# Where the last input forms of the gates and of the up projection are made, and at which offset the first weights of a block lie

## The chip, the cores and the metric

The kernel runs on one core of a Trainium2 chip. A core has TensorE (matmuls), VectorE, ScalarE, GpSimd and the queues that issue DMAs (SyncE's among them); each works through its own list of instructions in order, and they meet at semaphores. The metric is the device time of one execution in microseconds (us). The profile names the engines PE (its weight loads PEld), DVE, ACT, POOL and SP.

## The reference, cut to what matters

One layer of an encoder, 512 tokens of width 2048, all in float32:

```python
h = rmsnorm(x, norm_mix)
qa, ka, va, qb, kb, vb, ga, gb = split(h @ w_in)      # ga, gb: 2048 columns each
out_a = window_attention(...);  out_b = neighbourhood_attention(...)
merged = sigmoid(ga) * (out_a @ w_branch_a) + sigmoid(gb) * (out_b @ w_branch_b)
x = x + merged @ w_out
u = rmsnorm(x, norm_ffn) @ w_up                       # 2048 x 11264
u = depthwise_conv_of_width_3(u) + conv_b
gate, val = split(u)
x = x + (silu(gate) * val) @ w_down                   # 5632 x 2048
```

## The kernel before

**Precision.** A float32 number is kept as two parts of the type float32r: the high one (a cast on ScalarE) and the low one, what is left (a subtraction on VectorE). A product is made of three matmuls: high by high, high by low, low by high. So every 128-row tile of weights has to be split before TensorE can use it: L634 and L635 for the blocks described next, L735 and L736 for the others.

**Blocks of products.** From the fourth block of 512 gate columns on, the gates, the whole up projection and most of the down projection use seven products in place of eight: the work on two 128-row slices of the contraction, two halves of 256 columns and two halves of 256 tokens is taken as a 2 x 2 by 2 x 2 product, and seven sums of its quarters are multiplied (the method of Strassen and Winograd). One such piece is a *unit* (the class Product): 7 sums x 2 column tiles x 3 matmuls = 42 matmuls with 256 moving columns. Eight units, one for each pair of slices, make a block of up or of the gates, which holds seven PSUM banks. There are 5 blocks of gates (the first is called block 3), 22 of up, and 12 of down, of which 3 (PLAIN) go the ordinary way with all eight products. The weights' sums are partly made on VectorE (L589 to L593), partly fetched ready from DRAM.

**The forms of the input.** The other operand, seven sums of a pair of input slices, is called the pair's forms. They are made once and used by all blocks: eight pairs for the gates (hf, by form_h) and eight for up (h2, by form_pair). One pair costs one instruction of 512 and two of 256 columns on VectorE (L663, L665, L666), seven casts on ScalarE (L675) and seven subtractions on VectorE (L676), all of 256 columns. Before that, ScalarE scales the two slices by the norm's weights (L861 in scale_x, L976 in scale_pair). form_h(j) also has GpSimd issue the load of x's slices j + 2 (L854) and issues scale_x(j + 1). The seven forms lie in seven of 56 slots.

**Where the forms are made.** For the gates: while TensorE works on gate block 2, the last in the ordinary layout, whose input hT lies in the slots; before its steps 0 to 5 and 7, and the eighth pair after it (post_forms). For up: pairs 0 and 1 in the second quarter of the projection w_out, pairs 2 to 5 before steps 2, 4, 6 and 7 of its last quarter, and pairs 6 and 7 after it.

**Weights ahead of use.** When TensorE's matmuls of a unit have been issued, advance() issues the preparation (prep) of the unit two ahead: the first four sums ("a", L634 and L635 with 1024 columns), then the last three ("b", 768 columns). Each of these has two buffers, so the preparation waits until TensorE has read the unit before the last. The buffers of the first units of gates lie in the space of the older weight buffers (wst), which is closed at step 7 of gate block 2.

**The order of the instructions.** A planner writes each engine's list at compile time, by priority (the order in which the code issues) and by its own idea of when inputs are ready. An instruction wrapped in keep (tc.keep_in_program_order) is pinned behind the instruction that the code issued just before it on the same engine. The preparations and L663, L665 and L666 are pinned so; L675, L676, L861, L976, L837, L838 and what follows a block of w_out (L1000, L257, L258) are not.

**Offsets.** A weight buffer has 32 columns more than its weights need. In Product.prep the weights begin at column 28 for the first unit of a block (self.turn) and at column 16 for the others; a column has 4 bytes. Plain blocks use 16, the ordinary tiles 0 and 32.

Of the kernel before, what the change touches and what calls it, by code (L numbers as in the profile page):

```python
# [39 lines left out]
def trunk_kernel(  # L40
# [58 lines left out]
    for held, names in ((smalls, KEPT), (masks, SMALLS)):  # L99
        at = 0  # L100
# [17 lines left out]
    at = {"load": 0, "sums": 0, "prep": 0, "use": 0}  # L118

    def step(layout, w, cols, acts, evac, k0=0, nk=KD, before=None, pre=None, post=None, rate=RATE,  # L120
             unit=None):

        width = sum(n for _, n in cols)
        kpb = 1024 // width
        steps.append(partial(
            run_step, layout, kpb, width, nk, acts, evac, before, pre, post, rate))
        for k in range(0, nk, kpb):
            if unit is None:
                units.append(Plain(w, k0 + k, kpb, cols))
            else:  # L130
                (c, n), = cols
                view = w[(k0 + k) * P:(k0 + k + kpb) * P, c:c + n]
                units.append(unit(view.rearrange("(b p) n -> p b n", p=P), len(units)))
                products_.append(units[-1])

    class Plain:
# [18 lines left out]
        def prep(self, *between, pieces=1):  # L155
            self.load(pieces)
            for work in between:
                work()
            hi = wst["p"].tile([P, 1024], F32R, tag="hi", name="hi", bufs=2)
            lo = wst["p"].tile([P, 1024], F32R, tag="lo", name="lo", bufs=2)  # L160
            n = 1024 // pieces
            for c in range(0, 1024, n):
                nc.scalar.copy(hi[:, c:c + n], self.raw[:, c:c + n])  # L163
                nc.vector.tensor_tensor(  # L164
                    lo[:, c:c + n], self.raw[:, c:c + n], hi[:, c:c + n].bitcast(F32),
                    ALU.subtract)
            self.hi = hi.rearrange("p (a n) -> p a n", a=self.kpb)
            self.lo = lo.rearrange("p (a n) -> p a n", a=self.kpb)
# [377 lines left out]
    out_a = [dram.tile([P, S], F32, name=f"out_a{h}") for h in range(8)]  # L546
# [16 lines left out]
    class Product:  # L563
# [57 lines left out]
        def prep(self, *between):  # L621
            self.parts = []
            for b, (tag, n) in enumerate((("a", 4), ("b", 3))):
                if between:
                    between[b]()
                at = 28 if self.turn else 16
                hi, lo = (
                    ffn["w"].tile(
                        [P, n * 256 + 32], F32R, tag=f"{half}{tag}{self.first % 2}",
                        name="w" + half, bufs=1)[:, at:at + n * 256].rearrange(  # L630
                            "p (f n) -> p f n", f=n)
                    for half in "hl")
                f = self.f[:, 4 * b:4 * b + n]
                keep(nc.scalar.copy(hi, f))  # L634
                keep(nc.vector.tensor_tensor(lo, f, hi.bitcast(F32), ALU.subtract))  # L635
                self.parts += [(hi[:, i], lo[:, i]) for i in range(n)]
            for work in between[2:]:
                work()
# [30 lines left out]
    def forms(src):  # L669
        y, one, two = form_sums(src)  # L670
        all_ = y[:, 0], y[:, 2], two[:, 1], one[:, 1], one[:, 0], two[:, 0], y[:, 3]
        res = [slot(F32R) for _ in all_]
        for i in (0, 1, 6, 4, 3, 5, 2):
            v, o = all_[i], res[i]
            nc.scalar.copy(o[:, :256], v)  # L675
            nc.vector.tensor_tensor(o[:, 256:], v, o[:, :256].bitcast(F32), ALU.subtract)  # L676
        return res
# [33 lines left out]
    class Tiles:  # L711

        at = 0, 32
# [27 lines left out]
    class TilesByHalves(Tiles):  # L741
        at = 16, 16
# [86 lines left out]
    ra, merged, oa, ob, hf, held = {}, [None] * KD, [], [], [], {}  # L829
# [22 lines left out]
    def load_x(j):  # L852
        held[j] = quad("a")
        nc.gpsimd.dma_start(  # L854
            held[j], x_t[2 * j * P:(2 * j + 2) * P].rearrange("(a p) n -> p a n", p=P))

    def scale_x(j):
        if j < KD // 2:
            x = held[j]
            for i in range(2):  # L860
                nc.scalar.activation(  # L861
                    x[:, i], x[:, i], AF.Copy, scale=gmix[:, 2 * j + i:2 * j + i + 1])

    def form_h():

        j = len(hf)
        if j < KD // 2:
            hf.append(forms(held.pop(j)))
            if j + 2 < KD // 2:
                load_x(j + 2)  # L870
            scale_x(j + 1)
# [5 lines left out]
        scale_x(0)  # L877

    def before_forms(kb):
        if kb != 6:  # L880
            form_h()
        if kb == 7:
            wst_ctx.close()
            ffn["w"] = ctx.enter_context(tc.tile_pool(name="w", bufs=2, reuse_waits="tile"))
            ffn["limit"] = at["use"] + 1

    def post_forms():
        ffn["limit"] = len(units)
        prep_to(at["use"] + 1)
        form_h()  # L890

    def load_parts(src):

        hi, lo = slot(F32R), slot(F32R)
        dma(lo.bitcast(F32), src)
        return hi, lo
# [25 lines left out]
    def parts_behind(src, dst, first):  # L922

        def before(kb):
            n = 2 * (kb - first)
            if 0 <= n < 8:
                dst.extend(load_parts(o) for o in src[n:n + 2])
            for parts in dst[max(0, n - 2):max(0, n)]:
                split_parts(*parts)
        return before  # L930
# [27 lines left out]
    for blk in range(3, 8):  # L958
        gate_products(
            blk, kept=range(8) if blk == 3 else (1, 2),  # L960
            before=parts_behind(out_a, oa, 1) if blk == 7 else None)
    windows.append((len(units) + 2, len(units) + 64))
    for blk in range(4):
        branch(w_branch_a, blk, oa, gate_a, evac_a, before=parts_behind(out_b, ob, 0))
# [13 lines left out]
    def form_pair(j):  # L978
        if j not in scaled:
            scale_pair(j)  # L980
        h2[j] = forms(scaled.pop(j))

    def project_out(n):
        def pre():
            for m in range(4 * n, 4 * n + 4):
                x2[m] = slot()
                dma(x2[m], x_t[m * P:(m + 1) * P])

        def before(kb):
            if n == 1 and kb in (2, 5):  # L990
                form_pair(0 if kb == 2 else 1)
            if n == 2 and kb == 3:
                scale_pair(2)
                scale_pair(3)
            if n == 3 and kb in (2, 4, 6, 7):
                form_pair({2: 2, 4: 3, 6: 4, 7: 5}[kb])

        def evac(o, ps):
            m = 4 * n + o
            nc.vector.tensor_tensor(x2[m], ps, x2[m], ALU.add)  # L1000
            nc.gpsimd.dma_start(total[m // 2][:, m % 2], x2[m])
            square_sum("f", m, x2[m])

        def post():
            if n == 3:
                form_pair(6)
                form_pair(7)

        step("f", w_out, [(n * 512, 512)], merged, evac, pre=pre, before=before, post=post,
             unit=Tiles)  # L1010

    for n in range(4):
# [57 lines left out]
    def up(s):  # L1070
        def evac(gate, val):
            g, v = Conv(gate, 2 * s), Conv(val, 44 + 2 * s)
            made = []

            def silu():
                keep(nc.scalar.activation(g.o, g.o, AF.Silu))

            def out_part():
                keep(nc.vector.tensor_tensor(v.o, g.o, v.o, ALU.mult))
                made.extend(form_sums(v.o))  # L1080

            def store():
                y, one, two = made
                for o, x in ((0, y), (4, one), (6, two)):
                    keep(nc.scalar.dma_start(act[s][:, o:o + x.shape[1]], x))

            one, two, three = (unfinished.popleft() for _ in range(3))
            queue.extend((
                wait, lambda: (one(), scale(gate)), two,
                lambda: (three(), g.middle(), scale(val)), v.middle, wait, g.last, v.last))  # L1090
            unfinished.extend((silu, out_part, store))

        def before(i):
            if s == 0 and i == 4:
                rows["f"] = row_factor("f")
            if s == 0 and i == 7:
                rows["f"] = rows["f"]()[1]
            if s == pairs_ff - 1:
                load_act(0, i - 1)

        def after(i):
            if s == pairs_ff - 1:
                split_act(0, i - 6)

        view = w_up.rearrange("(d b p) (h n) -> d p b h n", b=2, p=P, h=2)
        products(view[:, :, :, :, s * 256:(s + 1) * 256], range(KD // 2), h2, evac,
                 before=before, after=after, kept=(2, 3, 7) if s else range(8))

    def down(part, n):
# [119 lines left out]
```

## Time and profile before

| | |
|---|---|
| median of 3 runs | 2491.49 us (2489.78 to 2492.13) |
| profiled execution, its own time | 2490.22 us |
| its span, first to last instruction | 2488.4 us |
| TensorE busy (PE) | 2453.3 us, 99% |
| VectorE busy (DVE) | 1908.4 us, 77% |
| ScalarE busy (ACT) | 1284.9 us, 52% |
| mean granted TensorE clock | 0.995 |

A row of a timeline has the start and the length in us, the engine, the line of the kernel, the operation, the tile written and the tiles read, the shape, the count of instructions merged into the row and, in brackets, how long the engine had been idle and what released it. A row of a group has the count, the busy time, the mean length of one in ns, and the idle time before them with its releasers. Instructions of one engine overlap a little, so a merged row of two is shorter than two rows. Matmuls overlap more: a matmul with 256 columns is listed with 278 ns, but one starts every 0.11 to 0.12 us. "wh" and "wl" are the high and low parts of weights, "s" is a slot.

### The profile page before, as it was taken

Reading aid. Unit: us, or ns where it says so; the run is one execution under the profiler, and the core shown is the slowest. Engines: PE = TensorE matmul, PEld = TensorE weight load, DVE = VectorE, ACT = ScalarE, POOL = GpSimd, SP = SyncE. Lnnn points to the kernel's source line nnn. Section 1 sums busy time; section 2 is a strip of 40 time slices with the busy share of each in tenths; the row PEclk is TensorE's granted clock in tenths of the full one; section 3 lists DMA queues with packets and bytes.
Section 4 is the critical chain, followed back from the end, with each engine's and each line's share of the span. In section 5 each row is a group of like instructions: output and inputs, shape, how many; then the busy total and the mean of one; then the engine's idle time right before and its main releaser. Section 6 shows DMA issues by size and latency. Waiting matters only on the chain.

```text
span 2488.4 us, 45723 instructions
## 1 busy us (share of the span) xinstructions
PE 2453.3 (99%) x17446; PEld 2292.0 (92%) x17446; DVE 1908.4 (77%) x3003; ACT 1284.9 (52%) x1954; POOL 327.2 (13%) x390
## 2 busy tenths in 40 slices
PE   9999999999999999999999999999999999999998
PEld 7888888888899888888999999999999999999998
DVE  6787677665788657556788888888888878697898
ACT  5354554355545323334566666666666666453633
POOL 1322123101000111111011110110111101000000
PEclk9999999999999999999999999999999999999999
DMA  5766667646555587777488888888888897776754
GB/s 199 257 228 212 231 215 238 213 134 203 173 171 168 192 279 244 234 239 235 142 219 221 216 235 222 223 228 218 231 220 216 232 280 193 207 192 171 226 156 133
DMA packets 340700, 525.46 MB, mean 211 GB/s; under 512 B 30720, under 2 KB 234112, under 8 KB 340480
## 3 DMA queue, kind: packets, MB, share of 16 engines
q1 hardware_dynamic: 254656, 319.70, 41.6%
q0 software_dynamic: 48384, 128.91, 21.6%
q10 hardware_dynamic: 37440, 73.94, 7.7%
q8 instruction: 136, 2.23, 0.4%
q14 instruction: 84, 0.69, 0.1%
HBM read 377.81 MB, written 98.57 MB: 191 GB/s over the span
## 4 chain that ended last, share of the span: by engine, by line
PE 92%; DVE 3%; DMA 2%; ACT 1%; issue 1%; SPq 0%; DVEq 0%; ACTq 0%; POOLq 0%
PE mm L78 88%; PE tr L78 2%; DMA f<-in_w_down 1%; PE tr L492 1%; DVE wl L635 1%; DVE s L1067 1%; ACT wh L634 0%; DVE s L676 0%; DMA s<-act 0%; DMA a<-in_x_t 0%; PE tr L350 0%; SPq L75 0%; DVE u L784 0%; DMA f<-sums 0%; ACT s L1066 0%
## 5 line engine op out<-in xcount | busy, mean ns | idle before, releaser
L78 PE MATMUL mm<-s,wh 128*128 128x256 f32 (+1 forms) x9620 | 1734.8, 290 | 14.9 <-ACT wh L634 11.5
L78 PEld LDWEIGHTS mm<-s,wh 128*128 128x128 f32 x9620 | 1443.6, 189 | 57.8 <-ACT wh L634 12.6
L78 PE MATMUL mm<-s,wl 128*128 128x256 f32 (+1 forms) x4810 | 1255.9, 289 | 3.3 <-DVE wl L635 3.3
L78 PEld LDWEIGHTS mm<-s,wl 128*128 128x128 f32 x4810 | 853.6, 188 | 24.5 <-DVE wl L635 4.4
L634 ACT CAST wh<-f 128x1024 fp32r<-128x1024 f32 (+1 forms) x566 | 517.3, 941 | 502.3 <-PE mm L78 359.1
L635 DVE TENSOR_TENSOR wl<-f,wh 128x1024 fp32r<-128x1024 f32 (+1 forms) x566 | 602.3, 1089 | 161.9 <-ACT wh L634 160.4
L78 PE MATMUL mm<-hi,s 128*128 128x512 f32 x896 | 286.3, 395 | 5.3 <-ACT hi L163 5.3
L736 DVE TENSOR_TENSOR wl<-f,wh 128x1024 fp32r<-128x1024 f32 x85 | 104.1, 1225 | 164.5 <-ACT wh L735 164.5
L735 ACT CAST wh<-f 128x1024 fp32r<-128x1024 f32 x85 | 89.2, 1050 | 237.6 <-PE mm L78 201.3
L78 PEld LDWEIGHTS mm<-hi,s 128*128 128x128 f32 x896 | 168.3, 189 | 38.2 <-ACT hi L163 5.3
L163 ACT CAST hi<-raw 128x1024 fp32r<-128x1024 f32 (+1 forms) x97 | 100.8, 1040 | 188.9 <-PE mm L78 140.9
L78 PE MATMUL mm<-s,hi 128*128 128x512 f32 x640 | 194.6, 392 | 2.4 <-ACT o L505 1.2
L164 DVE TENSOR_TENSOR lo<-raw,hi 128x1024 fp32r<-128x1024 f32 (+1 forms) x97 | 117.6, 1212 | 102.2 <-ACT hi L163 87.7
L78 PE MATMUL mm<-lo,s 128*128 128x512 f32 x448 | 176.9, 396 | 0.0
L78 PEld LDWEIGHTS mm<-s,hi 128*128 128x128 f32 x640 | 119.2, 188 | 26.4 <-ACT o L505 1.4
L589 DVE TENSOR_TENSOR f<-f 128x512 f32<-128x512 f32 x195 | 133.7, 686 | 0.0
L1036 POOL DMA_DIRECT2D o<-a x44 | 52.9, 1202 | 561.0 <-ACT a L1035 285.2
L78 PE MATMUL mm<-s,lo 128*128 128x512 f32 x320 | 118.8, 391 | 0.0
L609 DVE TENSOR_TENSOR s<-s 128x256 f32<-128x256 f32 x236 | 93.5, 421 | 14.6 <-DMA s<-in_w_up 12.1
L78 PEld LDWEIGHTS mm<-lo,s 128*128 128x128 f32 x448 | 84.6, 189 | 16.3
L1033 ACT ACTIVATE o<-u,smalls 128x512 f32<-128x512 f32 x88 | 71.2, 809 | 34.4 <-DVE t L666 30.2
L592 DVE TENSOR_TENSOR f<-f 128x256 f32<-128x256 f32 x195 | 83.0, 425 | 6.7
(148 smaller groups left out, 2047.7 us busy)
## 6 DMA issues: line engine op xcount, KB each, us to landing
f<-sums SPq DMA_DIRECT2D x88, 512.0 KB, 5.2
f<-in_w_up SPq DMA_DIRECT2D x176, 256.0 KB, 3.6
o<-a POOLq DMA_DIRECT2D x88, 511.0 KB, 7.2
f<-in_w_up SPq DMA_DIRECT2D x281, 128.0 KB, 3.6
raw<-in_w_in SPq DMA_DIRECT2D x63, 512.0 KB, 4.1
sums<-s ACTq DMA_DIRECT2D x118, 256.0 KB, 4.1
s<-in_w_up POOLq DMA_DIRECT2D x86, 256.0 KB, 5.1
s<-act SPq DMA_DIRECT2D x168, 128.0 KB, 4.2
```

What stands on the lines that cost most here:

```text
L78: return nc.tensor.matmul(o, l, r, start=start, stop=stop, skip_group_check=True).ins
L163: nc.scalar.copy(hi[:, c:c + n], self.raw[:, c:c + n])
L164: nc.vector.tensor_tensor(lo[:, c:c + n], self.raw[:, c:c + n], hi[:, c:c + n].bitcast(F32), ALU.subtract)
L589: keep(nc.vector.tensor_tensor(f[:, 3:5], f[:, 2::-2], f[:, 6].unsqueeze(1).to_broadcast([P, 2, 256]), ALU.add))
L592: keep(nc.vector.tensor_tensor(f[:, 5], f[:, 4], f[:, 2], ALU.add))
L609: add = lambda *args: keep(nc.vector.tensor_tensor(*args, ALU.add))
L634: keep(nc.scalar.copy(hi, f))
L635: keep(nc.vector.tensor_tensor(lo, f, hi.bitcast(F32), ALU.subtract))
L735: keep(nc.scalar.copy(hi, self.f))
L736: keep(nc.vector.tensor_tensor(lo, self.f, hi.bitcast(F32), ALU.subtract))
L1033: keep(nc.scalar.activation(self.o[:, m], u[:, m], AF.Identity, bias=cb[:, i:i + 1], scale=cw[:, i, 1:2]))
L1036: keep(nc.gpsimd.dma_start(self.o[:, :, 1:], first[:, :, :S - 1], accum_op=ALU.add))
```

## The change

The last two pairs of the gates' forms are issued within the first block of products, before its units 0 and 2, instead of before the last step of gate block 2 and after it. Pairs 5, 6 and 7 of up's forms are issued before units 0, 2 and 4 of up's first block, instead of before the last step of w_out and after it. And in a block's first unit only the last three sums begin at column 28; the first four begin at 16 as in other units.

```diff
@@ Product.prep
-                at = 28 if self.turn else 16
+                at = 28 if self.turn and b else 16
@@ before_forms
-        if kb != 6:
+        if kb < 6:
             form_h()
@@ post_forms
         ffn["limit"] = len(units)
         prep_to(at["use"] + 1)
-        form_h()
+
+    def last_forms(i):
+        if i in (0, 2):
+            form_h()
@@ the blocks of gates
         gate_products(
             blk, kept=range(8) if blk == 3 else (1, 2),
-            before=parts_behind(out_a, oa, 1) if blk == 7 else None)
+            before={3: last_forms, 7: parts_behind(out_a, oa, 1)}.get(blk))
@@ project_out, before
-            if n == 3 and kb in (2, 4, 6, 7):
-                form_pair({2: 2, 4: 3, 6: 4, 7: 5}[kb])
+            if n == 3 and kb in (2, 4, 6):
+                form_pair({2: 2, 4: 3, 6: 4}[kb])
@@ project_out
-        def post():
-            if n == 3:
-                form_pair(6)
-                form_pair(7)
-
-        step("f", w_out, [(n * 512, 512)], merged, evac, pre=pre, before=before, post=post,
+        step("f", w_out, [(n * 512, 512)], merged, evac, pre=pre, before=before,
              unit=Tiles)
@@ up, before
         def before(i):
+            if s == 0 and i in (0, 2, 4):
+                form_pair(5 + i // 2)
             if s == 0 and i == 4:
                 rows["f"] = row_factor("f")
```

## The prediction

> **What bounds the kernel now.** I read the busy shares first, then who kept TensorE waiting, then the two longest waits in order of time.
>
> ```profile
> PE 2453.3 (99%) x17446; PEld 2292.0 (92%) x17446; DVE 1908.4 (77%) x3003; ACT 1284.9 (52%) x1954; POOL 327.2 (13%) x390
> ...
> PE mm L78 <- ACT wh L634: 11.5, 3, 5.9
> PE mm L78 <- DVE wl L635: 3.3, 5, 0.8
> ```
>
> TensorE sets the time; of its waits, three for the high weight halves (L634) make 11.5 us. The timeline of TensorE has the two long ones: at the passage from gate block 2 into the first block of products (call it G), and in up's first block (U).
>
> ```profile
> 630.18 0.39 PE L78 MATMUL mm<-s,lo 128*128 128x512 f32 x1
> 634.88 3.36 PE L78 MATMUL mm<-s,wh 128*128 128x256 f32 x14 [4.31 <-ACT wh L634]
> 638.56 0.58 PE L78 MATMUL mm<-s,wl 128*128 128x256 f32 x1 [0.32 <-DVE wl L635]
> ...
> 640.91 0.40 PE L78 MATMUL mm<-s,wl 128*128 128x256 f32 x2
> ...
> 1187.60 0.28 PE L78 MATMUL mm<-s,wl 128*128 128x256 f32 x1
> 1193.78 3.35 PE L78 MATMUL mm<-s,wh 128*128 128x256 f32 x14 [5.89 <-ACT wh L634]
> 1196.93 0.35 PE L78 MATMUL mm<-s,wl 128*128 128x256 f32 x1
> 1197.12 0.40 PE L78 MATMUL mm<-s,wh 128*128 128x256 f32 x2
> ```
>
> Behind each wait 14 matmuls take 3.36 us, 0.24 each, twice what they take elsewhere. The windows by granted clock say why (columns: stretch, length, TensorE busy and its instructions, clock, DMA share, GB/s):
>
> ```profile
> 630.46:633.87 3.41, 0.11 (x1) 1.00 0.29 114
> 633.87:640.70 6.83, 5.50 (x24) 0.50 0.57 209
> 1186.83:1190.24 3.41, 1.05 (x9) 1.00 0.56 168
> 1190.24:1197.07 6.83, 3.29 (x15) 0.50 0.03 3
> 2029.92:2033.33 3.41, 1.97 (x11) 1.00 1.08 353
> 2033.33:2040.16 6.83, 5.78 (x25) 0.50 1.08 305
> 2374.71:2378.12 3.41, 2.18 (x19) 1.00 0.93 297
> ```
>
> A slice of 3.41 us with TensorE busy for 1.97 or less is followed by 6.83 us at half clock; one with 2.18 is not. So a wait costs itself and then up to 3.4 us. **G** loses this: the next matmul could have started at 630.41 (0.23 after 630.18); 25 matmuls lie before 640.91 and at 0.118 take 2.95, so they could be done at 633.36: 7.55 us lost. **U**: from 1187.72, 15 matmuls (1.77) would end at 1189.49; they end at 1197.12: 7.63 us lost.
>
> **What holds the weights up** at G: the instructions of ScalarE, VectorE and GpSimd.
>
> ```profile
> 628.27 0.72 POOL L854 DMA_DIRECT2D a<-in_x_t  x1 [6.55 <-ACT s L675]
> ...
> 632.56 1.33 ACT L861 ACTIVATE a<-a,gmix 128x512 f32<-128x512 f32 x2 [2.03 <-DMA a<-in_x_t]
> 633.80 1.76 ACT L634 CAST wh<-f 128x1024 fp32r<-128x1024 f32 x2
> ...
> 622.80 1.23 DVE L164 TENSOR_TENSOR lo<-raw,hi 128x1024 fp32r<-128x1024 f32 x1 [0.25 <-ACT hi L163]
> ...
> 633.37 0.70 DVE L837 TENSOR_TENSOR o<-mm,row 128x512 f32<-128x512 f32 x1
> 636.94 0.43 DVE L676 TENSOR_TENSOR s<-t,s 128x256 fp32r<-128x256 f32 x1 [2.87 <-ACT s L675]
> 637.28 2.09 DVE L635 TENSOR_TENSOR wl<-f,wh 128x1024 fp32r<-128x1024 f32 x2
> ```
>
> L634 and L635 are pinned behind what the code issued last on their engine. For the first unit of G that is form_h(6): ScalarE stands at scale_x(7) until the x tile issued at 628.27 lands (632.56), and VectorE until the last low part of pair 6 (636.94). At U they are pinned behind pairs 6 and 7:
>
> ```profile
> 1176.07 0.69 DVE L663 TENSOR_TENSOR t<-a 128x512 f32<-128x512 f32 x1
> ...
> 1182.28 2.10 DVE L635 TENSOR_TENSOR wl<-f,wh 128x1024 fp32r<-128x1024 f32 x2
> ...
> 1186.12 0.68 DVE L663 TENSOR_TENSOR t<-a 128x512 f32<-128x512 f32 x1
> ...
> 1192.81 0.43 DVE L676 TENSOR_TENSOR s<-t,s 128x256 fp32r<-128x256 f32 x1 [0.47 <-ACT s L675]
> 1193.75 4.10 DVE L635 TENSOR_TENSOR wl<-f,wh 128x1024 fp32r<-128x1024 f32 x4 [0.52 <-ACT wh L634]
> ...
> 1192.37 0.40 ACT L675 CAST s<-t 128x256 fp32r<-128x256 f32 x1 [0.94 <-DVE s L676]
> 1192.68 3.45 ACT L634 CAST wh<-f 128x1024 fp32r<-128x1024 f32 x4
> ```
>
> From 1186.12 to 1193.24 VectorE makes two pairs: 3.56 us for one. Only then unit 2's weights are split.
>
> **Part 1, G.** Nothing is removed; two form_h move, with their L663 to L676, scale_x(7) and the instructions that scale. The load of x tile 7 is issued by form_h(5) and stays. The first unit is now pinned behind L163/L164 (VectorE done at 624.03), so both halves, 2.1 us on each engine, are made under the last w_in unit: no wait at 630.41. The second unit is pinned behind the fourth gate's L837 and sigmoid (L838). TensorE ends that sum at about 630.6; L837 0.7, then a sigmoid of 0.63 (row below), then L634's 1.05 and 0.83: high halves at 633.0 and 633.9; low ones 1.22 and 0.95 on VectorE: 634.3 and 635.2. TensorE wants them at 630.41 + 42 x 0.118 = 635.37. That leaves 0.2. What can come late is scale_x(7): if it stands in ScalarE's queue before the fourth sigmoid, it again waits for the tile until 632.56 and everything is 2.5 us later: low half at 636.8, a wait of about 1.2. I take 1.0 of wait for G (ends: 0, and 1.4 + 3.4 if the slice falls under the limit). The third unit is pinned behind pair 6: from 635.2, 3.56 us for the pair and 1.22 for the first low half: 640.0, wanted at 635.37 + 4.9 = 640.3. Pair 7, made at unit 2, is used at unit 7; its x has landed by then. **Gain 7.55 - 1.0 = 6.55.**
>
> ```profile
> L634 ACT CAST wh<-f 128x1024 fp32r<-128x1024 f32 x283 | 296.9, 1049 | 350.7 <-PE mm L78 213.6 <-DVE f L589 63.7 <-issue 31.7
> L634 ACT CAST wh<-f 128x768 fp32r<-128x768 f32 x283 | 235.8, 833 | 151.6 <-PE mm L78 145.5 <-issue 3.5 <-DVE f L593 1.7
> L838 ACT ACTIVATE o<-o 128x512 f32<-128x512 f32 x4 | 2.4, 623 | 0.0
> ```
>
> **Part 2, U.** Pair 5 now stands behind the evacuation of w_out, and pairs 6 and 7 behind the preparations of units 3 and 5. Up to 1186.12 VectorE's work is the same as now (pair 5, the sums and squares of w_out, units 0 and 1), in another order; what follows is unit 2 and not pair 6. So its first low half is there at 1186.12 + 1.22 = 1187.35, the second at 1188.3; TensorE comes at 1187.72. I take 0.5 of wait (ends 0 and 1.5). After that pair 6 has from unit 3's split to unit 6, 9 us on, and a unit of 4.76 us (42 x 0.1133) needs 2.1 of VectorE's time: 2.7 are free in each, and weights are made two units ahead, so a pair of 3.56 is absorbed. If that cover were gone, each pair would cost 2.1 + 3.56 - 4.76 = 0.9. Pair 7 is needed at unit 7. **Gain 7.63 - 0.5 = 7.13.**
>
> **Part 3, the offset.** Now the weights of every block's first unit begin 28 elements in (112 bytes); all others at 16 or at multiples of 32. The windows of 30 steps each: the first two are first units, the third a later unit, the last a first unit of a plain block, whose weights sit at 16.
>
> ```profile
> 1264.31:1267.84 3.53, 3.53 (x32) 1.00 1.13 262
> 1302.62:1306.15 3.53, 3.53 (x32) 1.00 1.11 261
> 1278.14:1281.54 3.40, 3.40 (x32) 1.00 0.73 169
> 2144.92:2148.32 3.40, 3.40 (x32) 1.00 0.53 140
> ```
>
> Equal counts, 0.13 us apart: 4.3 ns a matmul. It goes by the offset, since the plain block's first unit is as fast as any later one. The change brings the first four sums, 24 of 42 matmuls, to 16. First units of products: 5 gate blocks, 22 of up, 12 - 3 of down: 36. 36 x 24 x 4.3 ns = **3.7 us** (ends 0 and 3.7). Where TensorE gets on 0.1 us sooner and meets an evacuation, it waits at most those 0.1, so no loss.
>
> **Sum.** The profiled execution took 2490.22 (span 2488.4 and 1.8 around it): 2490.2 - 6.55 - 7.13 - 3.7 = 2472.8. It lies 1.3 under the median of the runs, 2491.49; against that, **2474**.
>
> **By the Trainium skill**, page TensorE: Matmul & The Clock Gate, section What's actually happening, the clock falls after an idle window of about 3.4 us; by it a leftover wait of 1 to 2 us costs only itself, and case B below would be 2475. The trace differs: the slice at 2029.92, TensorE busy for 1.97 of 3.41 us, was followed by half clock.
>
> **The rivals.**
> A, as summed: 2474, own range 2470 to 2478 (the wait at the start of down, 2033.33, meets the slices of the clock at another phase; without its half clock up to 3 us less). 0.55.
> B, one wait stays long enough to halve the clock: scale_x(7) ahead of the last sigmoid, or unit 2 late at U because the casts of pair 5 queue. Wait 2 + 3.4 in place of 0.5 to 1.0: 2479. For it: ScalarE's 2.03 us at 632.56 shows that the written order takes the tile to be there sooner. Against: one miss alone gives 1.2. 0.20.
> C, the slow pitch belongs to a block's first unit and not to the address: no gain in part 3, 2477.8. Against it stands the plain block's row. Chance 0.12. The Trainium skill's page TensorE: Matmul & The Clock Gate, section Back-to-back issue gap, gives the gap from the moving size alone; by it, too, part 3 is worth nothing. The trace's 3.53 against 3.40 for equal counts differs.
> D, slower: pairs now stand between preparations five times (two at G, three at U), and each starves TensorE. It decides when a pair's 3.56 and the split's 2.1 don't fit before the unit two ahead is used; then five waits of 1.5 and five halved clocks, 5 x 4.9 = 24.5, eat gains of 7.55 + 7.63 + 3.7 = 18.9: 2497. Against: 2.7 us free per unit. 0.05.
> E, both waits are only shortened, with clocks halved at both, and the offset gives nothing (this is also the case that the change doesn't do what it says): 15.2 - 2 x 5.4 = 4.4 less: 2487. 0.08.
>
> **How the numbers follow.** A change under 0.2%, 5 us, is what a measurement can't tell from none. A, B and C are faster; of E nearly all is within 0.2%, D slower: faster 0.87, same 0.08, slower 0.05. The range takes A's lower end with the down wait unhalved, and goes up past B to B without the offset's 3.7: 2469 to 2483.
>
> **What would show it.** TensorE's waits on L634 fall from 11.5 to about 2; no half clock after 633 or 1187, one left at the start of down; L634 of the first gate unit starts before 630, L635 of up's unit 2 at about 1179 (1186.12 less what the gates gain); VectorE's forms stand between L635s. A first unit's first 24 matmuls take 2.72 us and not 2.82. If half clock remains at either place, or 3.53 stays, the sum is wrong there.

## The result, and the profile after

The changed kernel takes 2475.52 us (median; 2475.12 to 2476.53) against 2491.28 for the kernel before: a ratio of 0.9938, with a 95% interval from 0.9921 to 0.9955, or 15.8 us between the medians. The profiled execution took 2475.73 us, its span 2474.0. Forecast were 2474 and a range of 2469 to 2483; the time lies 1.5 us above the forecast, within rival A's own range.

From the page of the changed kernel the busy shares, and from its waits of TensorE those on weights and on L788, the copy with which ScalarE begins to empty a finished block's PSUM banks (us in all, times, longest):

```profile
PE 2445.2 (99%) x17446; PEld 2284.2 (92%) x17446; DVE 1907.7 (77%) x3003; ACT 1284.3 (52%) x1954; POOL 327.6 (13%) x390
```

```profile
PE mm L78 <- DVE wl L635: 3.4, 4, 1.1
PE mm L78 <- ACT wh L634: 3.1, 2, 1.8
...
PE mm L78 <- ACT t L788: 2.1, 1, 2.1
```

The counts of instructions are those of before; only where they stand has changed. The waits on L634 fell from 11.5 to 3.1 us; of these 3.1, 1.3 are a wait in the down projection that was there before.

The windows of the changed kernel by granted clock, at G, at the start of down, and at a stall among the attention's transposes (columns: stretch, length, busy time and instructions of PE, PEld, DVE, ACT and POOL, clock, DMA share, GB/s):

```profile
632.20:635.62 3.42, 2.08 (x17) 2.08 (x18) 3.31 (x5) 3.42 (x6) 0.57 (x1) 1.00 0.66 268
...
2018.04:2021.46 3.42, 1.57 (x9) 1.17 (x9) 1.59 (x5) 0.95 (x4) 0.00 (x0) 1.00 1.06 298
2021.46:2028.28 6.82, 5.30 (x25) 5.30 (x26) 5.49 (x7) 4.88 (x12) 0.00 (x0) 0.50 0.95 288
526.39:529.80 3.41, 1.78 (x14) 1.34 (x12) 2.26 (x3) 3.39 (x7) 0.00 (x0) 1.00 0.21 80
```

In this execution both half clocks at G and U are gone. The one at the start of down stays.

At **G** a wait is left. TensorE and ScalarE there in the changed kernel:

```profile
631.31 0.39 PE L78 MATMUL mm<-s,lo 128*128 128x512 f32 x1
633.54 1.91 PE L78 MATMUL mm<-s,wh 128*128 128x256 f32 x14 [1.84 <-ACT wh L634]
```

```profile
629.70 1.02 ACT L675 CAST s<-a 128x256 fp32r<-128x256 f32 x3
630.62 0.63 ACT L838 ACTIVATE o<-o 128x512 f32<-128x512 f32 x1
631.92 0.63 ACT L838 ACTIVATE o<-o 128x512 f32<-128x512 f32 x1 [0.67 <-DVE o L837]
632.46 1.76 ACT L634 CAST wh<-f 128x1024 fp32r<-128x1024 f32 x2
```

It is at the first unit, not at the second: the casts of pair 5 (the last three are shown) and two sigmoids went ahead of L634, which starts at 632.46, and the 14 matmuls on high halves then run at full clock (1.91 us for 14, as against 3.36). At **U** nothing is left. VectorE there, and TensorE's stretch in the chain that ended last (start, length):

```profile
1174.59 2.08 DVE L635 TENSOR_TENSOR wl<-f,wh 128x1024 fp32r<-128x1024 f32 x2
...
1177.99 0.68 DVE L663 TENSOR_TENSOR t<-a 128x512 f32<-128x512 f32 x1
...
1181.33 3.23 DVE L635 TENSOR_TENSOR wl<-f,wh 128x1024 fp32r<-128x1024 f32 x3 [0.42 <-ACT wh L634]
...
1186.77 0.68 DVE L663 TENSOR_TENSOR t<-a 128x512 f32<-128x512 f32 x1
```

```profile
645.06 547.50 PE mm L78 x3286
```

The pairs' L663 now stand between the L635s, and the chain stays on TensorE from 645 to 1193, through the place where it waited 5.89 us.

Both traces hold 17446 matmuls and transposes, in the same order but for 148 places in the first blocks behind G and U, so the k-th of one can be set against the k-th of the other. By how much the changed kernel starts it later (+) or sooner:

| place (time in the kernel before, us) | after - before, us | the stretch alone |
|---|---|---|
| before G, 628 | +1.13 | before the change: +1.13 |
| behind G, 690 | -4.26 | G: -5.39 |
| before U, 1186 | -4.78 | first units of gates: -0.52 |
| behind U, 1200 | -12.67 | U: -7.89 |
| end of up, 2020 | -14.83 | first units of up: -2.16 |
| in down, 2100 | -14.33 | start of down: +0.50 |
| end, 2470 | -14.49 | first units of down: -0.16 |

The first row is already +1.00 at 100 us, long before the first edit has any effect. The first 24 matmuls of a first unit of up take 2.72 us in the changed kernel and 2.83 in the kernel before (start to start, mean of 19 blocks).

### The profile page after: what moved, and what is told of

The parts are those of the page before. It is cut to its first block, busy times and chain, and to the rows that moved or that the text cites. A ratio compares the mean times of both kernels' runs of the same rounds, so it can differ in the third digit from the quotient of the medians.

```text
span 2474.0 us, 45724 instructions
## 1 busy us (share of the span) xinstructions
PE 2445.2 (99%) x17446; PEld 2284.2 (92%) x17446; DVE 1907.7 (77%) x3003; ACT 1284.3 (52%) x1954; POOL 327.6 (13%) x390
## 4 chain that ended last, share of the span: by engine, by line
PE 94%; DVE 2%; DMA 2%; ACT 1%; issue 1%; SPq 0%; DVEq 0%; ACTq 0%; POOLq 0%
PE mm L78 91%; PE tr L78 2%; PE tr L492 1%; DMA f<-in_w_down 1%; DMA raw<-in_w_in 1%; DMA a<-in_x_t 0%; DVE s L1065 0%; PE tr L350 0%; DVE wl L635 0%; DMA s<-act 0%; DVE s L676 0%; ACT wh L634 0%; SPq L75 0%; ACT hi L163 0%; DVE u L784 0%
## 5 line engine op out<-in xcount | busy, mean ns | idle before, releaser
L634 ACT CAST wh<-f 128x1024 fp32r<-128x1024 f32 (+1 forms) x566 | 516.5, 941 | 481.9 <-PE mm L78 320.5
L635 DVE TENSOR_TENSOR wl<-f,wh 128x1024 fp32r<-128x1024 f32 (+1 forms) x566 | 601.4, 1087 | 148.4 <-ACT wh L634 145.9
L163 ACT CAST hi<-raw 128x1024 fp32r<-128x1024 f32 (+1 forms) x97 | 101.0, 1041 | 194.0 <-PE mm L78 145.3
L164 DVE TENSOR_TENSOR lo<-raw,hi 128x1024 fp32r<-128x1024 f32 (+1 forms) x97 | 117.4, 1211 | 104.5 <-ACT hi L163 91.2
L78 PE MATMUL mm<-s,lo 128*128 128x512 f32 x320 | 118.7, 391 | 0.0
```

Of the source, the lines that this page charges most:

```text
L78: return nc.tensor.matmul(o, l, r, start=start, stop=stop, skip_group_check=True).ins
L164: nc.vector.tensor_tensor(lo[:, c:c + n], self.raw[:, c:c + n], hi[:, c:c + n].bitcast(F32), ALU.subtract)
```

## The experiments

### One part at a time

The offset alone, on the kernel before:

```diff
-                at = 28 if self.turn else 16
+                at = 28 if self.turn and b else 16
```

> The kernel before with part 3 alone: the first four sums of a block's first unit begin at column 16, the forms stay where they were. By the address (my step): 36 first units x 24 matmuls x 4.3 ns = 3.7 us less, 2487.6 against 2491.3; the waits at 630 and 1188 and their half clocks stay. By rival C (the slow pitch belongs to the first unit and not to the address): 2491.3, unchanged, and the first 24 matmuls of a first unit still go at 118 ns.

Measured: 2488.62 us against 2491.2, 2.6 less where 3.7 were expected, ratio 0.9987 (0.9978 to 0.9996). Set against the kernel before matmul by matmul, up's blocks bring 2.25 us from 1200 to 2020. The gain is there without either of the other parts, so rival C falls.

The gates' forms alone:

```diff
-        if kb != 6:
+        if kb < 6:
             form_h()
...
-        form_h()
+
+    def last_forms(i):
+        if i in (0, 2):
+            form_h()
...
+            before={3: last_forms, 7: parts_behind(out_a, oa, 1)}.get(blk))
```

> The kernel before with part 1 alone: the last two pairs of the gates' forms within the first block of products. By my step 6.55 us less. The trace of the changed kernel shows 1.84 us of wait left at the first unit, in place of 1.0 at the second, and no half clock: 7.55 - 1.84 = 5.7 less, 2485.6. By rival E (wait only shortened, clock halved all the same) 2.2 less, 2489.

Measured: 2486.53 us, 4.7 less, ratio 0.9983 (0.9974 to 0.9992). The profiled execution, 2491.48, is the longest of the eleven, so its trace shows what can happen and not what usually does. In it the wait at G is as long as with all parts (1.81 us, and 1.84 there), yet here the clock is halved behind it. TensorE's row, and the windows by clock:

```profile
634.31 2.35 PE L78 MATMUL mm<-s,wh 128*128 128x256 f32 x14 [1.81 <-ACT wh L634]
```

```profile
632.18:635.59 3.41, 1.60 (x12) 1.28 (x11) 3.31 (x6) 2.90 (x5) 0.57 (x1) 1.00 0.77 251
635.59:639.00 3.41, 3.41 (x18) 3.41 (x17) 1.56 (x2) 3.35 (x6) 0.56 (x1) 0.50 0.50 158
```

The same wait lies in a slice with TensorE busy for 2.08 us in the one trace and for 1.60 in the other, because the program came 0.8 us later to it (632.11 for the last matmul of gate block 2, and 631.31) while the slice begins at the same time in both (632.18 and 632.20). Half the clock for 3.41 us then costs 1.7: G brought 3.6 us here (from +1.93 at 628 to -1.63 at 690), against 5.4. The traces of the kernels with eight offsets and with everything shifted (below), which keep the wait at G, show half clock behind it too: from 633.76, for 3.41 us, behind slices with TensorE busy for 1.51 and 1.39 us.

Up's forms alone:

```diff
-            if n == 3 and kb in (2, 4, 6, 7):
-                form_pair({2: 2, 4: 3, 6: 4, 7: 5}[kb])
+            if n == 3 and kb in (2, 4, 6):
+                form_pair({2: 2, 4: 3, 6: 4}[kb])
...
-            if n == 3:
-                form_pair(6)
-                form_pair(7)
...
+            if s == 0 and i in (0, 2, 4):
+                form_pair(5 + i // 2)
```

> The kernel before with part 2 alone: pairs 5, 6 and 7 of up's forms within up's first block. By my step 7.1 us less; with no wait left at all, as the changed kernel's trace shows, 7.6 less, 2483.7. If the gain at this place needed the shift that the other parts bring, less than 6. The half clock at 1190 is gone, those at 634 and 2033 stay.

Measured: 2482.24 us, 9.0 less, ratio 0.9966 (0.9953 to 0.9978). Matmul by matmul U brings 7.90 us, from +2.90 at 1186 to -5.00 at 1200; here too the profiled execution, 2485.75, is the longest, with half clock at the attention's stall (from 530.60). The chain that ended last runs through the place on TensorE alone:

```profile
641.91 558.32 PE mm L78 x3370
```

The three ratios multiply to 0.9936; all parts together have 0.9938. The parts add up as far as these intervals tell, and none needs another.

### Which of up's pairs held unit 2

On the changed kernel with column 16 for all units (next section), pair 5 goes back before the last step of w_out:

```diff
-            if n == 3 and kb in (2, 4, 6):
-                form_pair({2: 2, 4: 3, 6: 4}[kb])
+            if n == 3 and kb in (2, 4, 6, 7):
+                form_pair({2: 2, 4: 3, 6: 4, 7: 5}[kb])
...
-            if s == 0 and i in (0, 2, 4):
+            if s == 0 and i in (2, 4):
```

> Column 16 for all units, and pair 5 of up's forms stays before the last step of w_out; pairs 6 and 7 stand before units 2 and 4 of up's first block. By my step only pairs 6 and 7 held up unit 2, so the wait at U stays away and the time is that of column 16 alone, 2472.3 within 0.5. If moving pair 5 was needed as well, a wait on L634 or L635 of 1 us or more in up's first three units, with up to 3.4 of half clock: 2473.5 to 2477.

Measured: 2472.57 us (2471.24 to 2475.11), against 2472.33 for the kernel that it differs from in this alone. U has no wait; in the chain that ended last TensorE runs on through it:

```profile
643.65 547.26 PE mm L78 x3286
```

So moving pairs 6 and 7 is enough, and moving pair 5 earns nothing that shows.

### What the slow pitch hangs on

Column 16 for every unit of the products:

```diff
-                at = 28 if self.turn and b else 16
+                at = 16
```

> The changed kernel with column 16 for every unit, so the last three sums of a first unit too lose the odd offset. If the pitch goes by the address alone, 36 x 18 x 4.3 ns = 2.8 us less than the changed kernel: 2472.7. If the odd offset of these sums helps something else, no gain or a loss against 2475.5.

Measured: 2472.33 us (2471.49 to 2473.08), 3.2 less than the changed kernel; the odd offset that the change keeps for the last three sums only costs. Matmul by matmul up's 21 blocks (1200 to 2020) gain 2.54 us more than in the changed kernel, 0.12 a block, where 18 x 4.3 ns make 0.08. The planner issues 12 of these 18 in two groups of six among the second unit's matmuls, and there they cost some 8 ns each: the second unit takes 4.76 us in place of 4.85. Why they cost more there no run shows.

Then eight offsets, each for an eighth of the units:

```diff
-                at = 28 if self.turn and b else 16
+                at = 4 * (self.first // 2 % 8)
```

> The changed kernel with the weights of unit n of the products at column 4 x (n // 2 mod 8), so at byte 0, 16, 32, 48, 64, 80, 96 or 112, each for an eighth of the 283 units. By my step the pitch belongs to the address: matmuls at byte 64 go at 113.5 ns and those at 112 at 117.8, first units or not. If only 112 is slow, 283 x 42 / 8 x 4.3 ns = 6.4 us more than with 64 everywhere (the kernel with column 16 for all, 2472.3): 2479. If all that are no multiple of 32 bytes are slow, 26 us more: 2498; if all that are no multiple of 64, 38 more: 2511. By rival C only first units are slow and the eight bytes differ by nothing.

Measured: 2521.27 us, in one execution, 49 more than with column 16, and more than any of the three cases expected. The start-to-start times of its matmuls with 256 columns (those with a gap of over 145 ns left out), grouped by the byte of the weights' address modulo 128:

| byte | 0 | 16 | 32 | 48 | 64 | 80 | 96 | 112 |
|---|---|---|---|---|---|---|---|---|
| mean, ns | 119.2 | 118.4 | 118.4 | 118.4 | 113.8 | 118.7 | 118.2 | 117.8 |
| matmuls | 1495 | 1510 | 1592 | 1596 | 2442 | 1427 | 1385 | 1383 |

Not 112 is slow; 64 is fast, and it alone. (Byte 64 has more matmuls because the plain blocks keep column 16.) In the built program the inputs of all these matmuls lie at byte 0, so this leaves two readings: the weights' own byte, or its distance from the input's. The next two kernels shift slots and weight buffers together by 64 bytes; a smaller tile ahead of them does it. The first keeps column 16, so the distance stays 64 and the weights come to byte 0:

```diff
-FILL, EDGE = 124, 120
+FILL, EDGE = 108, 120
```

> Column 16 for all units, and all that lies behind the fill tile moved 64 bytes down, the slots of the inputs' forms and the weight buffers alike: inputs begin at byte 64 of a 128-byte line, weights at byte 0. If the weights' own byte decides (only 64 is fast), all 283 x 42 matmuls go at 118.5 ns in place of 113.4: 60 us more, 2532. If the distance from the weights to the input decides, it is 64 as before: 113.4 ns and 2472.

Measured: 2472.04 us, in one execution. The second has column 0 on top of it, so that both begin at byte 64:

```diff
-FILL, EDGE = 124, 120
+FILL, EDGE = 108, 120
...
-                at = 16
+                at = 0
```

> The same shift with column 0 for the products' units: inputs and weights both begin at byte 64. If the weights' own byte decides, 113.4 ns and 2472 (the plain blocks, which keep column 16 and so come to byte 0, may cost some 5 more). If the distance decides, it is 0 now: 118.5 ns or more and 2532.

Measured: 2529.51 us, in one execution. The windows of 100 us of steady work in up (TensorE's busy time and its matmuls come first), in this order: column 16 for all, eight offsets, both shifted with column 16, both shifted with column 0:

```profile
1400.00:1500.00 100.00, 100.00 (x885) 100.00 (x884) 87.89 (x115) 63.45 (x84) 10.80 (x9) 1.00 0.85 224
```

```profile
1400.00:1500.00 100.00, 100.00 (x851) 100.00 (x850) 82.08 (x108) 65.47 (x87) 14.41 (x12) 1.00 0.85 221
```

```profile
1400.00:1500.00 100.00, 100.00 (x884) 100.00 (x884) 87.59 (x115) 63.33 (x83) 10.80 (x9) 1.00 0.83 222
```

```profile
1400.00:1500.00 100.00, 100.00 (x843) 100.00 (x842) 82.14 (x108) 64.51 (x85) 13.45 (x12) 1.00 0.84 218
```

With the weights at byte 0 and the inputs at 64 a matmul starts every 113.4 ns; with both at 64, every 118.9 (start to start, as in the table; a window's count takes in the two or three matmuls that run across its start, so 100 us by 884 and by 843 give a little less). TensorE shows 100% busy and the full clock in all four rows; only the count tells. With inputs at byte 0, weights at 64 are fast and at 0 slow; with inputs at 64 it is the other way round. So it is the distance between the two operands that decides: 64 bytes modulo 128 is fast, and the other distances tried cost 4 to 5.4 ns a matmul. The six distances besides 0 and 64 were tried with inputs at byte 0 alone. In the plain blocks of the last kernel, where column 16 now means byte 0 and a distance of 64 again, matmuls go at 113.8 ns.

### The wait left at G

With column 16 for all, the four sigmoids (and nothing else) are pinned:

```diff
+        pin = keep if first else lambda i: i
...
-        nc.scalar.activation(s, s, AF.Sigmoid)
+        pin(nc.scalar.activation(s, s, AF.Sigmoid))
...
-        gate(m, ps, held["g"][:, m % 2])
+        gate(m, ps, held["g"][:, m % 2], True)
```

> Column 16 for all units, and the four sigmoids of the last ordinary gate block pinned behind the first unit's L634. If the wait left at G comes from the sigmoids that stand ahead of L634 on ScalarE, L634 starts at once behind the casts of pair 6, some 1.8 us sooner, and what is late next is L635, behind the four L837 on VectorE: the wait on L634 falls from 1.4 to under 0.3, one on L635 of 0.5 to 1.3 appears. If L634 waits for its inputs or its buffer, it starts no sooner and the wait stays at 1.4.

Measured: 2471.95 us, in one execution, which can't be told from the 2472.33 without the pin; the traces tell. ScalarE and TensorE at G, first with column 16 alone:

```profile
632.62 0.63 ACT L838 ACTIVATE o<-o 128x512 f32<-128x512 f32 x1 [0.97 <-DVE o L837]
633.16 1.76 ACT L634 CAST wh<-f 128x1024 fp32r<-128x1024 f32 x2
```

```profile
634.24 1.92 PE L78 MATMUL mm<-s,wh 128*128 128x256 f32 x14 [1.27 <-ACT wh L634]
```

Then with the pin (the sigmoid is L839 here):

```profile
630.39 1.01 ACT L675 CAST s<-a 128x256 fp32r<-128x256 f32 x3
631.32 1.78 ACT L634 CAST wh<-f 128x1024 fp32r<-128x1024 f32 x2
633.00 1.15 ACT L839 ACTIVATE o<-o 128x512 f32<-128x512 f32 x2
```

```profile
633.36 1.81 PE L78 MATMUL mm<-s,wh 128*128 128x256 f32 x14
635.85 0.39 PE L78 MATMUL mm<-s,wl 128*128 128x256 f32 x1 [0.68 <-DVE wl L635]
```

Right behind pair 5's casts L634 could run at once: its inputs and its buffer were there by then, and only the order of the list had held it. What is late next is the low half, as expected, by 0.68 us; L635 stands behind the four L837.

Then pair 5 too goes into the first block, and with it its own casts leave ScalarE's list ahead of L634 (the expectations here and above call them the casts of pair 6; counted from 0, as elsewhere, it is pair 5, the sixth to be made):

```diff
-        if kb < 6:
+        if kb < 5:
             form_h()
...
-        if i in (0, 2):
+        if i in (0, 2, 4):
             form_h()
```

> As the one with pinned sigmoids, and pair 5 of the gates' forms too is made within the first block (three pairs before units 0, 2 and 4). The casts of pair 6 no longer stand ahead of the first unit's L634: it starts at about 628.5 and TensorE finds the high halves ready; left is up to 1 us on L635 behind L837. Against column 16 alone (2472.3) a gain of 0.5 to 1.4: 2471.4. If a third pair within the block starves a later unit (rival D in small), a new wait on L634 or L635 between 640 and 665 and 2473 or more.

Measured: 2469.65 us (2469.51 to 2470.4), ratio 0.9912 (0.9897 to 0.9927) to the kernel before: the fastest of all that ran, below the changed kernel's 2475.12 to 2476.53 and column 16 alone with 2471.49 to 2473.08. At G, on ScalarE, VectorE and TensorE:

```profile
626.79 1.76 ACT L634 CAST wh<-f 128x1024 fp32r<-128x1024 f32 x2
```

```profile
632.12 4.09 DVE L635 TENSOR_TENSOR wl<-f,wh 128x1024 fp32r<-128x1024 f32 x4
```

```profile
631.31 1.81 PE L78 MATMUL mm<-s,wh 128*128 128x256 f32 x14
633.39 0.38 PE L78 MATMUL mm<-s,wl 128*128 128x256 f32 x1 [0.27 <-DVE wl L635]
```

Here L634 does start before 630, and 0.27 us of wait is left; no later unit waits for its weights up to 700, so the third pair starves none. The medians differ from column 16 alone by 2.7 us, the two profiled executions by 1.9. Set against each other matmul by matmul, this kernel is 1.5 ahead before G (628), gains 1.4 at G (2.92 ahead at 690) and loses 1.0 behind it. Only the 1.4 lies where the two kernels' source differs. Ahead of G it is column 16 alone that loses 2.5 us between 500 and 600, with half clock at the attention's stall (from 530.93), where this trace has none.

## Why the prediction was right, and where not

**The sum.** It gave 2472.8 for one profiled execution and 2474 for the median; 2475.5 came. By its terms, from the table of matmuls: G -5.39 for -6.55, U -7.89 for -7.13, the offset about -2.8 (0.52 + 2.16 + 0.16) for -3.7, and the start of down +0.50, which the sum didn't have; with the +1.13 before G that makes 2475.7, the profiled execution. U's surplus of 0.8 hid part of what G and the offset fell short, by chance.

**G: the place was wrong.** The step that failed is "The first unit is now pinned behind L163/L164 ..., so both halves ... are made under the last w_in unit: no wait at 630.41". A pin says only behind what an instruction must stand, not how soon it comes. The planner put the unpinned casts of pair 5 and two sigmoids ahead of L634, and it started at 632.46, where the sign was "before 630". The kernel with pinned sigmoids (631.32) and the one that moves pair 5 as well (626.79) show that this order is what held it. The second unit, for which I took 1.0 us, had no wait: scale_x(7) came behind L634 and found its tile there. 1.84 at the first unit for 1.0 at the second is most of the term's error of 1.2.

**U was right,** and better than taken. Unit 2's L635 was to start at 1186.12 in the time of before; the matmuls before U come 4.78 us sooner, which makes 1181.34, and it started at 1181.33. My own two times (low half at 1187.35, wanted at 1187.72) left 0.37 to spare; the 0.5 us of wait that I still took wasn't needed. The sign "at about 1179" was off by some 2 us: half of it the +1.13 before G, half what G and the gates' first units brought less than their terms (5.9 for about 7). That VectorE's work up to there is nearly the same whether pair 5 comes early or late is borne out by the kernel in which pair 5 stays: in the time of the kernel before, its L635 of unit 2 starts at 1186.7, and at 1186.2 with column 16 alone. Rival D (each pair between preparations starves TensorE) and rival E fall with the missing waits.

**The offset: the price was right, the reason too narrow.** 24 matmuls by 4.3 ns is 0.103 us a block, and 21 blocks of up brought 2.16, or 0.103 each. Rival C falls by the kernel with the offset alone and by the eight offsets. But "It goes by the offset" is only half of it: it goes by the weights' distance from the input, and 16 is the one good column of the eight tried because the inputs begin at byte 0. The term was too large by about 0.9, all of it outside up's later blocks: the first units of block 3 and of up's first block lie in places where waits were, and down's nine product blocks brought 0.16 in place of 0.9. That down's waits for L635 (3.4 us in the whole trace) take back what the sooner matmuls gain there is my reading, and no run tests it. It fits that these waits, between the same matmuls of down (2100 to 2470 in the kernel before), make 3.0 us there, 3.4 in the changed kernel and 3.6 with the offset alone; that is about half of what is missing in the changed kernel.

The Trainium skill's page TensorE: Matmul & The Clock Gate, section Back-to-back issue gap, has the gap depend on the moving size; the rows with 884 and 843 matmuls of one size in 100 us disagree with that as a full account.

**The clock.** That a wait at G or U costs itself and half a clock on top held. The limit that I read (busy 1.97 of 3.41 us halves, 2.18 doesn't) isn't one number: 1.97 halved in the kernel before, while the slice with 1.78 in the changed kernel was followed by full clock. Nor is the half clock's length one number: 6.83 us in the rows of before, 3.41 behind the slice with 1.60 in the kernel with the gates' forms alone. What decides stays open. Rival B's mechanism, a wait that halves the clock, did show in that experiment and in two later traces. That the changed kernel's profiled execution escaped it at G, with 2.08, was a matter of 0.8 us of phase, so luck; my "ends: 0, and 1.4 + 3.4" for this place held both.

The Trainium skill's page TensorE: Matmul & The Clock Gate, section What's actually happening, speaks of an idle window of about 3.4 us; the rows with 1.60, and with 1.57 at the start of down, show half clock behind windows in which TensorE worked for nearly half of the time.

**The start of down.** One half clock stays there, as said. The wait on L788 grew from 0.9 to 2.1 us, and the offset alone moves it to 1.3, as the waits of the kernel before and of that with the offset alone have it:

```profile
PE mm L78 <- ACT t L788: 0.9, 1, 0.9
```

```profile
PE mm L78 <- ACT t L788: 1.3, 1, 1.3
```

I had allowed for another phase there only as a gain of up to 3; it was a loss of 0.5.

## What to carry to other kernels

Work that is due later but issued first holds up everything pinned behind it; look at what an urgent instruction is pinned behind, and move the pairs, tiles or forms that aren't needed yet to behind it. Then read the list that the planner made, since unpinned work can still go ahead. And where a matmul's pitch differs at full clock and 100% busy, compare the counts in equal windows and then the addresses of its two operands modulo 128.

## What had not been expected

The two operands of a 256-column matmul in float32r run at 113.4 to 113.8 ns a matmul when the weights begin 64 bytes, modulo 128, from the input, and at 117.8 to 119.2 at the seven other distances tried. Over the 283 units of 42 matmuls that is some 57 us (2529.51 against 2472.04), over three and a half times what the whole change brought. Why 64 is good no run shows.
